# Block loads on GpSimd's DMA queue, an act's transposes inside the down product, and other paces for the side pieces

## The chip, the cores and the metric

One core of one Trainium2 chip runs the kernel. The metric is the device time of one execution in microseconds (us); the median of several runs counts. 0.2% of it is 3.9 us.

## The reference, cut to what matters

A transformer layer stack on 256 tokens of width 2048, in float32: a mixer (gated linear attention and dilated attention), a feed-forward part, a second mixer (retention and convolution), and a sliding-window attention. The change touches the feed-forward part alone:

```python
D_MODEL = 2048; SEQ = 256; FFN_HIDDEN = 5632
h = rms_norm(x, g2)
act = silu(h @ w_gate) * (h @ w_up)      # w_gate, w_up: 2048 x 5632
x = x + act @ w_down                     # w_down: 5632 x 2048
```

## The kernel before, in words

**Products.** A float32 product is made of three TensorE products: each operand is split into a high and a low half (`split`, L162 on ScalarE casts the high half `hi`, L163 on VectorE subtracts to get the low half `lo`), and `three` (L187 to L189) adds x_hi·w_hi, x_hi·w_lo and x_lo·w_hi into one PSUM bank. "A half" below is such a `lo` row on VectorE (DVE). Weights come from HBM in raw tiles of 128 x 2 x 512 (512 KB, five of them, `rows` at L126 issues them on SyncE's queue, SP); four `hi` and four `lo` tiles. `linear` makes an output block of 256 x 512: 8 steps for every 512 rows of the weight, each step one call of `three` for one of the two 128-row halves of the tokens, and after each step a call of `deal()`.

**The feed-forward part** goes over 11 column blocks of 512 (NB). `plain(j)` computes column block j by `linear` over w_gate and w_up: SiLU of the first product, then the product row L556 (twice, one for each 128 tokens) makes the act, and `act_done` transposes it (8 transposes, L545, into PSUM tiles `tr`) and splits it into the operand pair `mh`, `ml` of the down product. `seven(j)` computes another column block by a scheme of seven block products in place of eight; its work isn't called at once but put into a queue of side pieces, `side`, from which `deal()` takes one every `pace[0]` steps of the running `linear`: 12 `first` pieces (a raw load, split, products) and then 16 `rest` pieces. A `rest` piece subtracts one 128 x 2 x 512 block of weights from another in place (L668, on DVE), splits the result and multiplies. `ahead` loads these blocks into a ring of six tiles (two named b in the raw pool, two in the pool of the act pairs, u10 and u11), one to two pieces ahead: a block's load can be issued only when the last reader of the tile six blocks earlier, a half on DVE, is through. The result banks of `rest` are the PSUM tiles named `at` and one `acc`.

**The order.** There are five rounds: `seven(2w+1)` fills the queue, `plain(2w+2)` runs (64 steps), and `down` (64 steps) multiplies two acts by w_down in four column blocks (`x_add`, L254, adds them to x), the side pieces being dealt into all of it; `drain` runs what is left. One round is 128 steps. The tile framework's scheduler then sets the final order on each engine from the program's order and its dependences; the excerpts below are of that final order. In it, u10 and u11 are printed as `u_...` and the first four tiles of the ring as `b_...`, with a running number.

Of the kernel before, what the change touches and what calls it, by code (L numbers as in the profile page):

```python
# [18 lines left out]
P = 128  # L19
# [61 lines left out]
def model(ctx, tc, a, out):  # L81
    nc = tc.nc
# [14 lines left out]
    def nm(s):  # L97
        cnt[0] += 1
        return f"{s}{cnt[0]}"
# [4 lines left out]
    def unit(i, shape, dtype=F32):  # L104
        return wk.tile([P] + list(shape), dtype, tag=f"u{i}", name=nm(f"u{i}_"))
# [15 lines left out]
    def raw_tile():  # L121
        return raw_p.tile([P, 2, 512], F32, tag="raw", name=nm("raw"))

    def rows(dst, w, k, c0, n=512):

        nc.sync.dma_start(dst[:, :, :n], w[k * P:(k + 2) * P, c0:c0 + n].rearrange("(k p) f -> p k f", p=P))  # L126

    def fetch(w, kg, c0, n):

        raws = [raw_tile() for _ in range(2)]  # L130
        for i in range(2):
            rows(raws[i], w, 4 * kg + 2 * i, c0, n)
        return raws
# [26 lines left out]
    def split(hi, lo, src, scale=None):  # L160
        if scale is None:
            A.copy(hi, src)  # L162
            V.tensor_tensor(lo, src, hi.bitcast(F32), ALU.subtract)  # L163
        else:
            A.activation(hi, src, AF.Copy, scale=scale)
            V.scalar_tensor_tensor(lo, src, scale, hi.bitcast(F32), ALU.mult, ALU.subtract)

    def pair(pool, tag, **kw):
        return (pool.tile([P, 4, S], F32R, tag=tag + "h", name=nm(tag + "h"), **kw),
                pool.tile([P, 4, S], F32R, tag=tag + "l", name=nm(tag + "l"), **kw))  # L170
# [6 lines left out]
    pace = [1, 0]  # L177

    def deal():
        if side:  # L180
            pace[1] += 1
            if pace[1] >= pace[0]:
                pace[1] -= pace[0]
                side.popleft()()

    def three(o, xh, xl, hi, lo, start, stop):
        T.matmul(o, xh, hi, start=start, stop=False)  # L187
        T.matmul(o, xh, lo, start=False, stop=False)  # L188
        T.matmul(o, xl, hi, start=False, stop=stop)  # L189

    def linear(w, c0, n, groups, got=(), fine=False):
        accs = [ps_acc.tile([P, 512], F32, tag="acc", name=nm("acc")) for _ in range(2)]
        for gi, ((xh, xl), kg) in enumerate(groups):
            raws = got[gi] if gi < len(got) else fetch(w, kg, c0, n)
            for k in range(4):
                k2 = k % 2
                if k2 == 0:
                    raw = raws[k // 2]
                    hi = hl_p.tile([P, 2, 512], F32R, tag="hi", name=nm("hi"))
                    lo = hl_p.tile([P, 2, 512], F32R, tag="lo", name=nm("lo"))  # L200
                    if fine and gi == 0:
                        for j in range(2):
                            split(hi[:, j, :n], lo[:, j, :n], raw[:, j, :n])
                    else:
                        split(hi[:, :, :n], lo[:, :, :n], raw[:, :, :n])
                for t in range(2):
                    o = accs[t][:, :n]
                    st, en = gi == 0 and k == 0, gi == len(groups) - 1 and k == 3
                    sl = slice(t * P, (t + 1) * P)
                    three(o, xh[:, k, sl], xl[:, k, sl], hi[:, k2, :n], lo[:, k2, :n], st, en)  # L210
                    deal()
        return accs
# [35 lines left out]
    def full(st):  # L248
        return [(st["T"][b], b) for b in range(4)]

    def x_add(b, accs):
        for t in range(2):
            xs = x[:, t, b * 512:(b + 1) * 512]
            V.tensor_tensor(xs, xs, accs[t], ALU.add)  # L254
# [61 lines left out]
    for b in range(4):  # L316
        xh, xl = st["T"][b] = pair(xt_p, "x")
# [13 lines left out]
    got = first  # L331
    for c0, n in ((2688, 400), (2304, 384), (2048, 256)):
        accs = linear(w_in, c0, n, full(st), got, fine=n == 400)
        got = []
# [91 lines left out]
    for vb in range(2):  # L426
# [4 lines left out]
        for hh in range(2):  # L431
# [19 lines left out]
            for t in range(2):  # L451
                o = po[:, t * S:(t + 1) * S]
                T.matmul(o, aT[:, t], v[:, t, vs], start=True, stop=True)
                for c in range(2):
                    n = 2 * t + c
# [69 lines left out]
    w_gate, w_up, w_down = a["w_gate"][0], a["w_up"][0], a["w_down"][0]  # L525
# [3 lines left out]
    acts = {}  # L529
    nst = new_stream()  # L530

    def down(bs, last):
        for b in range(4):
            x_add(b, linear(w_down, b * 512, 512, [(acts[j], j) for j in bs]))
            if last:
                x_done(nst, b, NEV)

    def act_done(j, sg):
        ah, al = acts[j] = pair(mt_p, "m")
        for i in range(2):  # L540
            ps = ps_w.tile([P, 512], F32, tag="w", name=nm("tr"))
            for k in range(2):
                for t in range(2):
                    c = (2 * i + k) * P
                    T.transpose(ps[:, k * S + t * P:k * S + (t + 1) * P], sg[:, t, c:c + P], ident)  # L545
            split(ah[:, 2 * i:2 * i + 2].rearrange("p c s -> p (c s)"),
                  al[:, 2 * i:2 * i + 2].rearrange("p c s -> p (c s)"), ps)

    def plain(j):
        ag = linear(w_gate, j * 512, 512, full(st))  # L550
        sg = unit(4, [2, 512])
        for t in range(2):
            silu_gate(sg[:, t], ag[t], rh[:, t:t + 1])
        au = linear(w_up, j * 512, 512, full(st))
        for t in range(2):
            V.scalar_tensor_tensor(sg[:, t], au[t], r2h[:, t:t + 1], sg[:, t], ALU.mult, ALU.mult)  # L556
        act_done(j, sg)

# [66 lines left out]
    def seven(j):  # L627

        c0 = j * 512
        c = {}  # L630

        def first(kp, n):
            if kp == 0:
                c[n] = work_bank()
            raw = raw_tile()
            rows(raw, (w_gate, w_up, w_gate)[n], (0, 8, 8)[n] + 2 * kp, c0)
            times(c[n], ("A11", "S4", "A12")[n], parts(raw), kp)
            if n == 2:
                ahead(0, kp)
            if kp < 3:  # L640
                return
            if n < 2:
                c["p", n] = temp("Lx", 4)
                A.copy(c["p", n], c[n])
                return
            sg = c["sg"] = unit(5, [2, 512])
            c11 = temp("junk2", 3)
            V.tensor_tensor(c11, c["p", 0], c[2], ALU.add)
            silu_gate(sg[:, 0], c11, rh[:, 0:1])

        def ahead(kp, n):

            if kp > 3:
                return
            for i in ((0, 1), (), (2,), (3,))[n]:
                b = c["b", kp, i] = block_tile()
                rows(b, (w_up, w_gate, w_up, w_gate)[i], (0, 0, 8, 8)[i] + 2 * kp, c0)

        def rest(kp, n):
            ahead(kp + 1, n)  # L660
            if n == 0:
                if kp == 0:
                    pace[0] = 5.75
                    c["P"] = [work_bank() for _ in range(3)] + [ps_acc.tile([P, 512], F32, tag="acc", name=nm("acc"))]
            b12, b11, b22, b21 = [c["b", kp, i] for i in range(4)]
            dst, x0, x1, which = ((b11, b12, b11, "S1"), (b12, b22, b12, "S3"), (b22, b22, b11, "S2"),
                                  (b21, b22, b21, "A22"))[n]
            V.tensor_tensor(dst, x0, x1, ALU.subtract)  # L668
            times(c["P"][n], which, parts(dst), kp)
            if kp == 3 and n == 3:  # L670
                last()

        def last():
            b5, b7, b6, b4 = c["P"]
            p1, p3, sg = c["p", 0], c["p", 1], c["sg"]
            V.tensor_tensor(p1, p1, b6, ALU.add)
            c12, c21 = temp("junk2", 3), temp("junk2", 3)
            V.tensor_tensor(c12, p1, b5, ALU.add)
            V.tensor_tensor(p1, p1, b7, ALU.add)
            V.tensor_tensor(c21, p1, b4, ALU.subtract)  # L680
            V.tensor_tensor(p1, p1, b5, ALU.add)
            V.tensor_tensor(c12, c12, p3, ALU.add)
            silu_gate(sg[:, 1], c21, rh[:, 1:2])
            for t, cu in enumerate((c12, p1)):
                V.scalar_tensor_tensor(sg[:, t], cu, r2h[:, t:t + 1], sg[:, t], ALU.mult, ALU.mult)
            act_done(j, sg)


        pace[0] = 1.75
        side.extend([lambda kp=kp, n=n: first(kp, n) for kp in range(4) for n in range(2)])  # L690
        side.extend([lambda kp=kp: first(kp, 2) for kp in range(4)])
        side.extend([lambda kp=kp, n=n: rest(kp, n) for kp in range(4) for n in range(4)])

    def drain():
        while side:
            side.popleft()()
        pace[0] = 1

    plain(0)
    left_sums()  # L700
    for w in range(5):
        seven(2 * w + 1)
        plain(2 * w + 2)
        down([2 * w - 1, 2 * w + 2] if w else [0, 2], False)
        drain()
    down([9], True)
    st = nst
# [74 lines left out]
    for half in range(2):  # L782
# [15 lines left out]
        for c in range(4):  # L798
            i = 4 * half + c
# [202 lines left out]
    for g in range(4):  # L1002
# [4 lines left out]
        sg = unit((0, 4)[g % 2], [2, 512])  # L1007
# [53 lines left out]
```

## Time and profile before

| | |
|---|---|
| median of 3 runs | 1927.17 us (1927.04 to 1930.02) |
| the profiled execution | 1926.19 us, its span 1924.4 us |
| TensorE (PE) busy | 1906.0 us, 99% |
| VectorE (DVE) busy | 1276.6 us, 66% |
| ScalarE (ACT) busy | 968.9 us, 50% |
| GpSimd (POOL) busy | 201.1 us, 10% |
| bytes read from HBM | 384 MB, 201 GB/s over the span |

Times in the profile are counted from the start of the span. The feed-forward part lies between about 400 and 1105 us. A row of the timeline gives the start, the time, the engine, the line of the kernel, the operation with its output and inputs, and in brackets how long the engine stood idle before it and what ended the wait. The views used are the busy table, the busy time in a window, the lists of waits by engine, the timelines of single engines, the times from issue to landing of one tile's DMAs, and the list of DMA issues.

### The profile page before, as it was taken

Reading aid. Unit: us, or ns where it says so; the run is one execution under the profiler, and the core shown is the slowest. Engines: PE = TensorE matmul, PEld = TensorE weight load, DVE = VectorE, ACT = ScalarE, POOL = GpSimd, SP = SyncE. Lnnn points to the kernel's source line nnn. Section 1 sums busy time; section 2 is a strip of 40 time slices with the busy share of each in tenths; the row PEclk is TensorE's granted clock in tenths of the full one; section 3 lists DMA queues with packets and bytes.
Section 4 is the critical chain, followed back from the end, with each engine's and each line's share of the span. In section 5 each row is a group of like instructions: output and inputs, shape, how many; then the busy total and the mean of one; then the engine's idle time right before and its main releaser. Section 6 shows DMA issues by size and latency. Waiting matters only on the chain.

```text
span 1924.4 us, 23805 instructions
## 1 busy us (share of the span) xinstructions
PE 1906.0 (99%) x8808; PEld 1567.0 (81%) x8808; DVE 1276.6 (66%) x1486; ACT 968.9 (50%) x1313; POOL 201.1 (10%) x315
## 2 busy tenths in 40 slices
PE   8999999999999999999999999999999999999999
PEld 8877888888778888788787888888888888878787
DVE  6454555587787887787887875555555666677654
ACT  6544545465546546455455454444444354566542
POOL 1000222110000000000000110100000003754100
PEclk9999999999999999999999999999999999999999
DMA  8675665567768778677687656566666556544464
GB/s 306 198 209 152 186 175 165 166 207 249 247 223 276 233 227 272 221 259 240 229 268 238 191 165 192 159 196 169 191 188 191 191 179 188 170 132 132 146 202 134
DMA packets 202724, 387.72 MB, mean 201 GB/s; under 512 B 12312, under 2 KB 20528, under 8 KB 202480
## 3 DMA queue, kind: packets, MB, share of 16 engines
q1 hardware_dynamic: 201472, 382.12, 64.3%
q0 software_dynamic: 992, 4.03, 0.7%
q8 instruction: 69, 1.13, 0.2%
q14 instruction: 47, 0.39, 0.1%
q10 hardware_dynamic: 144, 0.05, 0.0%
HBM read 384.04 MB, written 3.68 MB: 201 GB/s over the span
## 4 chain that ended last, share of the span: by engine, by line
PE 89%; DMA 4%; DVE 4%; issue 1%; POOL 1%; ACT 0%; SPq 0%; DVEq 0%; ACTq 0%
PE acc L188 25%; PE acc L187 25%; PE acc L189 25%; PE at L188 2%; PE at L189 2%; PE at L187 2%; DVE lo L163 2%; DMA b<-in_w_up_dram 2%; DMA b<-in_w_gate_dram 1%; PE at L960 1%; DVE b L668 1%; DMA u<-in_w_up_dram 1%; PE tr L225 1%; PE tr L307 1%; DMA u<-in_w_gate_dram 0%
## 5 line engine op out<-in xcount | busy, mean ns | idle before, releaser
L163 DVE TENSOR_TENSOR lo<-raw,hi 128x1024 fp32r<-128x1024 f32 (+3 forms) x646 | 786.4, 1224 | 464.8 <-ACT hi L162 460.2
L162 ACT CAST hi<-raw 128x1024 fp32r<-128x1024 f32 (+3 forms) x646 | 669.4, 1040 | 664.8 <-PE acc L189 561.5
L188 PE MATMUL acc<-lo,xh 128*128 128x512 f32 (+3 forms) x1640 | 637.2, 389 | 0.4 <-DVE lo L163 0.4
L189 PE MATMUL acc<-hi,xl 128*128 128x512 f32 (+3 forms) x1640 | 636.2, 388 | 0.0
L187 PE MATMUL acc<-hi,xh 128*128 128x512 f32 (+3 forms) x1640 | 622.7, 390 | 5.7 <-ACT hi L162 5.7
L187 PEld LDWEIGHTS acc<-hi,xh 128*128 128x128 f32 x1640 | 308.2, 188 | 68.8 <-ACT hi L162 6.0
L188 PEld LDWEIGHTS acc<-lo,xh 128*128 128x128 f32 x1640 | 308.9, 188 | 64.1 <-issue 3.3
L189 PEld LDWEIGHTS acc<-hi,xl 128*128 128x128 f32 x1640 | 309.0, 188 | 59.5 <-issue 0.4
L188 PE MATMUL acc<-lo,mh 128*128 128x512 f32 x640 | 251.0, 392 | 0.0
L189 PE MATMUL acc<-hi,ml 128*128 128x512 f32 x640 | 249.0, 393 | 0.0
L187 PE MATMUL acc<-hi,mh 128*128 128x512 f32 x640 | 247.1, 393 | 1.0 <-ACT mh L162 1.0
L187 PEld LDWEIGHTS acc<-hi,mh 128*128 128x128 f32 x640 | 120.5, 188 | 27.1 <-DVE x L254 1.5
L188 PEld LDWEIGHTS acc<-lo,mh 128*128 128x128 f32 x640 | 120.3, 188 | 25.7 <-DVE lo L163 1.8
L189 PEld LDWEIGHTS acc<-hi,ml 128*128 128x128 f32 x640 | 119.8, 188 | 24.4
L162 ACT CAST hi<-b 128x1024 fp32r<-128x1024 f32 x54 | 56.9, 1054 | 74.5 <-PE acc L189 47.3
L163 DVE TENSOR_TENSOR lo<-b,hi 128x1024 fp32r<-128x1024 f32 x54 | 65.9, 1221 | 4.8 <-ACT hi L162 3.9
L668 DVE TENSOR_TENSOR b<-b,b 128x1024 f32<-128x1024 f32 x41 | 50.1, 1222 | 28.3 <-DMA b<-in_w_gate_dram 13.5
L720 POOL DMA_DIRECT2D u<-in_c_even_dram x1 | 0.6, 633 | 651.9 <-PE at L189 651.9
L254 DVE TENSOR_TENSOR x<-x,acc 128x512 f32<-128x512 f32 x88 | 57.7, 681 | 9.9 <-PE acc L189 9.8
L188 PE MATMUL at<-lo,u 128*128 128x512 f32 x160 | 63.5, 397 | 0.4 <-DVE lo L163 0.3
L189 PE MATMUL at<-hi,u 128*128 128x512 f32 x160 | 62.4, 390 | 0.0
L187 PE MATMUL at<-hi,u 128*128 128x512 f32 x160 | 62.4, 390 | 0.0
(253 smaller groups left out, 1567.1 us busy)
## 6 DMA issues: line engine op xcount, KB each, us to landing
raw<-in_ev_w_in_dram SPq DMA_DIRECT2D x128, 512.0 KB, 3.9
raw<-in_w_gate_dram SPq DMA_DIRECT2D x88, 512.0 KB, 4.5
raw<-in_w_down_dram SPq DMA_DIRECT2D x88, 512.0 KB, 5.1
raw<-in_w_in_dram SPq DMA_DIRECT2D x80, 512.0 KB, 3.8
raw<-in_od_w_in_dram SPq DMA_DIRECT2D x72, 512.0 KB, 3.7
raw<-in_w_up_dram SPq DMA_DIRECT2D x68, 512.0 KB, 4.7
raw<-in_w_out_dram SPq DMA_DIRECT2D x32, 512.0 KB, 3.6
raw<-in_ev_w_out_dram SPq DMA_DIRECT2D x32, 512.0 KB, 3.7
```

What stands on the lines that cost most here:

```text
L162: A.copy(hi, src)
L163: V.tensor_tensor(lo, src, hi.bitcast(F32), ALU.subtract)
L187: T.matmul(o, xh, hi, start=start, stop=False)
L188: T.matmul(o, xh, lo, start=False, stop=False)
L189: T.matmul(o, xl, hi, start=False, stop=stop)
L225: T.transpose(ps[:, k * S + t * P:k * S + (t + 1) * P], x[:, t, c:c + P], ident)
L254: V.tensor_tensor(xs, xs, accs[t], ALU.add)
L307: T.transpose(ps[:, k * S + t * P:k * S + (t + 1) * P], src(t)[:, c:c + P], ident)
L668: V.tensor_tensor(dst, x0, x1, ALU.subtract)
L720: nc.gpsimd.dma_start(ce, a["c_even"][:, :512])
L960: T.matmul(pv[e * 64:(e + 1) * 64, :S], vo[:, k, g * 64:(g + 1) * 64], PT[:, :, e], start=k == 0, stop=k == t)
```

## The change

`rows` takes the queue as an argument, and `ahead` issues its blocks on GpSimd's queue, in the program's order. `plain` no longer transposes its act: it returns a function, which `down` calls (as `mid`) in its first column block before the second group of eight steps. `down` reads `acts[j]` when it comes to the group. The paces become 2.5 steps for the `first` pieces and 5.1 for the `rest` pieces (1.75 and 5.75 before). The rows L556, L545, L668 and L254 of before are L559, L548, L672 and L257 in the changed kernel.

```diff
@@ -121,9 +121,9 @@
     def raw_tile():
         return raw_p.tile([P, 2, 512], F32, tag="raw", name=nm("raw"))
 
-    def rows(dst, w, k, c0, n=512):
-
-        nc.sync.dma_start(dst[:, :, :n], w[k * P:(k + 2) * P, c0:c0 + n].rearrange("(k p) f -> p k f", p=P))
+    def rows(dst, w, k, c0, n=512, queue=nc.sync):
+
+        return queue.dma_start(dst[:, :, :n], w[k * P:(k + 2) * P, c0:c0 + n].rearrange("(k p) f -> p k f", p=P))
 
     def fetch(w, kg, c0, n):
 
@@ -188,9 +188,12 @@
         T.matmul(o, xh, lo, start=False, stop=False)
         T.matmul(o, xl, hi, start=False, stop=stop)
 
-    def linear(w, c0, n, groups, got=(), fine=False):
+    def linear(w, c0, n, groups, got=(), fine=False, mid=None):
         accs = [ps_acc.tile([P, 512], F32, tag="acc", name=nm("acc")) for _ in range(2)]
-        for gi, ((xh, xl), kg) in enumerate(groups):
+        for gi, (pr, kg) in enumerate(groups):
+            if gi == 1 and mid is not None:
+                mid()
+            xh, xl = pr() if callable(pr) else pr
             raws = got[gi] if gi < len(got) else fetch(w, kg, c0, n)
             for k in range(4):
                 k2 = k % 2
@@ -529,9 +532,9 @@
     acts = {}
     nst = new_stream()
 
-    def down(bs, last):
+    def down(bs, last, mid=None):
         for b in range(4):
-            x_add(b, linear(w_down, b * 512, 512, [(acts[j], j) for j in bs]))
+            x_add(b, linear(w_down, b * 512, 512, [(lambda j=j: acts[j], j) for j in bs], mid=mid if b == 0 else None))
             if last:
                 x_done(nst, b, NEV)
 
@@ -554,7 +557,7 @@
         au = linear(w_up, j * 512, 512, full(st))
         for t in range(2):
             V.scalar_tensor_tensor(sg[:, t], au[t], r2h[:, t:t + 1], sg[:, t], ALU.mult, ALU.mult)
-        act_done(j, sg)
+        return lambda: act_done(j, sg)
 
 
 
@@ -654,13 +657,14 @@
                 return
             for i in ((0, 1), (), (2,), (3,))[n]:
                 b = c["b", kp, i] = block_tile()
-                rows(b, (w_up, w_gate, w_up, w_gate)[i], (0, 0, 8, 8)[i] + 2 * kp, c0)
+                tc.keep_in_program_order(rows(b, (w_up, w_gate, w_up, w_gate)[i], (0, 0, 8, 8)[i] + 2 * kp, c0,
+                                              queue=nc.gpsimd))
 
         def rest(kp, n):
             ahead(kp + 1, n)
             if n == 0:
                 if kp == 0:
-                    pace[0] = 5.75
+                    pace[0] = 5.1
                     c["P"] = [work_bank() for _ in range(3)] + [ps_acc.tile([P, 512], F32, tag="acc", name=nm("acc"))]
             b12, b11, b22, b21 = [c["b", kp, i] for i in range(4)]
             dst, x0, x1, which = ((b11, b12, b11, "S1"), (b12, b22, b12, "S3"), (b22, b22, b11, "S2"),
@@ -686,7 +690,7 @@
             act_done(j, sg)
 
 
-        pace[0] = 1.75
+        pace[0] = 2.5
         side.extend([lambda kp=kp, n=n: first(kp, n) for kp in range(4) for n in range(2)])
         side.extend([lambda kp=kp: first(kp, 2) for kp in range(4)])
         side.extend([lambda kp=kp, n=n: rest(kp, n) for kp in range(4) for n in range(4)])
@@ -696,12 +700,12 @@
             side.popleft()()
         pace[0] = 1
 
-    plain(0)
+    plain(0)()
     left_sums()
     for w in range(5):
         seven(2 * w + 1)
-        plain(2 * w + 2)
-        down([2 * w - 1, 2 * w + 2] if w else [0, 2], False)
+        mid = plain(2 * w + 2)
+        down([2 * w - 1, 2 * w + 2] if w else [0, 2], False, mid)
         drain()
     down([9], True)
     st = nst
```

**Place 1, DVE in the first round, around the product row.** In the kernel before (the `lo` rows are halves of blocks, b_ and u_, and of raw tiles):

```order
L668 TENSOR_TENSOR u_890_4346<-u_885_4314,u_890_4346 128x1024
L163 TENSOR_TENSOR lo_4334<-raw_4301,hi_4333 128x1024
L163 TENSOR_TENSOR lo_4350<-b_4189,hi_4349 128x1024
L163 TENSOR_TENSOR lo_4387<-raw_4382,hi_4386 128x1024
L163 TENSOR_TENSOR lo_4403<-raw_4383,hi_4402 128x1024
L668 TENSOR_TENSOR b_4411<-b_4409,b_4411 128x1024
L556 SCALAR_TENSOR_TENSOR u_848_4133<-acc_4138,r2h_3443,u_848_4133 128x512
L556 SCALAR_TENSOR_TENSOR u_848_4133<-acc_4139,r2h_3443,u_848_4133 128x512
L163 TENSOR_TENSOR lo_4415<-b_4234,hi_4414 128x1024
```

and in the changed kernel:

```order
L672 TENSOR_TENSOR u_887_4336<-u_887_4336,b_4267 128x1024
L163 TENSOR_TENSOR lo_4358<-raw_4353,hi_4357 128x1024
L672 TENSOR_TENSOR u_898_4380<-u_887_4336,u_898_4380 128x1024
L163 TENSOR_TENSOR lo_4374<-raw_4354,hi_4373 128x1024
L559 SCALAR_TENSOR_TENSOR u_838_4103<-acc_4108,r2h_3443,u_838_4103 128x512
L559 SCALAR_TENSOR_TENSOR u_838_4103<-acc_4109,r2h_3443,u_838_4103 128x512
L163 TENSOR_TENSOR lo_4384<-b_4225,hi_4383 128x1024
L163 TENSOR_TENSOR lo_4423<-raw_4418,hi_4422 128x1024
L163 TENSOR_TENSOR lo_4438<-b_4267,hi_4437 128x1024
L163 TENSOR_TENSOR lo_4454<-raw_4419,hi_4453 128x1024
L672 TENSOR_TENSOR b_4434<-b_4432,b_4434 128x1024
L163 TENSOR_TENSOR ml_4403<-tr_4404,mh_4402 128x512
```

Before, the two product rows (L556) stood behind the subtraction of b_4411; now they (L559) stand ahead of the subtraction of b_4434, and behind this one stands the half of the transposed act (ml_4403).

**Place 2, TensorE (PE) in the same stretch, around the act's transposes.** Before (acc_4380 and acc_4381 are the down product's banks, at_4068 one of the `rest` products):

```order
L187 MATMUL acc_4380<-hi_4402,mh_3745 128x512
L188 MATMUL acc_4380<-lo_4403,mh_3745 128x512
L189 MATMUL acc_4380<-hi_4402,ml_3746 128x512
L187 MATMUL at_4068<-hi_4414,u_763_3789 128x512
L545 MATMUL tr_4366<-cm,u_848_4133 128x128
L187 MATMUL acc_4381<-hi_4386,mh_3745 128x512
```

and in the changed kernel (acc_4352 is a bank of the down product, acc_4128 of the `rest` products):

```order
L187 MATMUL acc_4352<-hi_4373,mh_3745 128x512
L188 MATMUL acc_4352<-lo_4374,mh_3745 128x512
L189 MATMUL acc_4352<-hi_4373,ml_3746 128x512
L548 MATMUL tr_4404<-cm,u_838_4103 128x128 x4
L188 MATMUL acc_4128<-lo_4384,xh_3310 128x512
L189 MATMUL acc_4128<-hi_4383,xl_3311 128x512
L187 MATMUL acc_4128<-hi_4383,xh_3310 128x512
```

The first transpose stood 13 matmuls behind the first matmul of the down product; it now stands 25 matmuls behind it, with 31 matmuls between it and the last of the up product (18 before).

**Place 3, the queues that issue the block loads, first round.** SP before:

```order
L126 DMA u_885_4314<-in_w_up_dram 128x2x512
L126 DMA raw_4433<-in_w_down_dram 128x2x512
L126 DMA raw_4434<-in_w_down_dram 128x2x512
L126 DMA b_4409<-in_w_up_dram 128x2x512
L126 DMA raw_4484<-in_w_down_dram 128x2x512
L126 DMA b_4411<-in_w_gate_dram 128x2x512
L126 DMA raw_4485<-in_w_down_dram 128x2x512
```

and GpSimd (POOL) in the changed kernel:

```order
L126 DMA u_887_4336<-in_w_up_dram 128x2x512
L126 DMA u_898_4380<-in_w_gate_dram 128x2x512
L126 DMA b_4432<-in_w_up_dram 128x2x512
L126 DMA b_4434<-in_w_gate_dram 128x2x512
L126 DMA b_4504<-in_w_up_dram 128x2x512
L126 DMA b_4544<-in_w_gate_dram 128x2x512
```

The blocks stood among the raw loads on SP; now they follow one another on GpSimd's queue, and SP issues raw loads alone.

## Rows read from the trace of the kernel before

**Rows 1.** The page: span, busy time of each engine, TensorE's granted clock in 40 slices.

```profile
span 1924.4 us, 23805 instructions
...
PE 1906.0 (99%) x8808; PEld 1567.0 (81%) x8808; DVE 1276.6 (66%) x1486; ACT 968.9 (50%) x1313; POOL 201.1 (10%) x315
...
PEclk9999999999999999999999999999999999999999
```

**Rows 2.** Windows: the feed-forward part, busy time (instructions) by engine, clock, DMA share, GB/s.

```profile
400.00:1110.00 710.00, 703.27 (x3127) 575.29 (x3126) 571.70 (x568) 374.00 (x391) 14.39 (x24) 1.00 0.74 238
```

**Rows 3.** Waits of PE, 400 to 1100 us: total us, times, longest us.

```profile
PE tr L545 <- DVE u L556: 5.3, 4, 1.9
PE at L188 <- DVE lo L163: 0.3, 1, 0.3
```

**Rows 4.** Timeline of DVE, 505 to 580 us: start, us, row, idle before it.

```profile
515.94 1.23 DVE L668 TENSOR_TENSOR b<-u,b 128x1024 f32<-128x1024 f32 x1 [3.12 <-DMA u<-in_w_up_dram]
...
518.35 1.22 DVE L163 TENSOR_TENSOR lo<-b,hi 128x1024 fp32r<-128x1024 f32 x1
...
521.75 1.22 DVE L163 TENSOR_TENSOR lo<-b,hi 128x1024 fp32r<-128x1024 f32 x1
...
528.53 1.23 DVE L668 TENSOR_TENSOR b<-b,b 128x1024 f32<-128x1024 f32 x1 [3.29 <-DMA b<-in_w_gate_dram]
...
539.97 1.23 DVE L668 TENSOR_TENSOR b<-b,b 128x1024 f32<-128x1024 f32 x1 [2.33 <-DMA b<-in_w_up_dram]
541.12 1.22 DVE L163 TENSOR_TENSOR lo<-u,hi 128x1024 fp32r<-128x1024 f32 x1
...
568.24 1.22 DVE L163 TENSOR_TENSOR lo<-raw,hi 128x1024 fp32r<-128x1024 f32 x1
...
577.64 1.22 DVE L163 TENSOR_TENSOR lo<-raw,hi 128x1024 fp32r<-128x1024 f32 x1
```

**Rows 5.** Timeline of PE, places between 520 and 580 us.

```profile
520.50 0.39 PE L188 MATMUL at<-lo,u 128*128 128x512 f32 x1
...
524.29 0.39 PE L188 MATMUL acc<-lo,xh 128*128 128x512 f32 x1
...
542.39 0.50 PE L188 MATMUL at<-lo,u 128*128 128x512 f32 x1 [0.29 <-DVE lo L163]
...
569.51 0.50 PE L188 MATMUL acc<-lo,mh 128*128 128x512 f32 x1
...
578.99 0.42 PE L188 MATMUL acc<-lo,mh 128*128 128x512 f32 x1
```

**Rows 6.** Waits of SP's queue, 400 to 1100 us.

```profile
SPq L126 <- DVE lo L163: 549.6, 311, 6.9
```

**Rows 7.** Timeline of SP's queue, 505 to 525 us.

```profile
508.96 0.37 SPq L126 DMA_DIRECT2D raw<-in_w_down_dram  x1
510.09 0.37 SPq L126 DMA_DIRECT2D u<-in_w_up_dram  x1
...
523.00 0.37 SPq L126 DMA_DIRECT2D b<-in_w_gate_dram  x1
```

**Rows 8.** Timeline of all engines, 160 to 163 us: DVE and GpSimd.

```profile
161.23 0.88 DVE L281 SCALAR_TENSOR_TENSOR og<-at,fq,u 128x256 f32<-128x256 f32 x2 [2.44 <-ACT u L430]
...
162.41 0.87 POOL L466 DMA_DIRECT2D u<-skew  x1 [1.21 <-DVE og L281]
```

**Rows 9.** Tile u, 161 to 167 us: its DMA (GpSimd's load of the skewed tile).

```profile
DMA to landing us min/median/max: 4.2/4.2/4.2
```

**Rows 10.** Tile raw, 155 to 159 us: its DMAs (SP).

```profile
DMA to landing us min/median/max: 3.6/3.7/3.8
```

**Rows 11.** DMA issues, whole span: tile, queue, count, KB each, median us to landing.

```profile
raw<-in_w_in_dram SPq DMA_DIRECT2D x80, 512.0 KB, 3.8
...
b<-in_w_up_dram SPq DMA_DIRECT2D x27, 512.0 KB, 4.9
...
u<-skew POOLq DMA_DIRECT2D x2, 512.0 KB, 4.8
```

## The prediction, made before the changed kernel was run

> **What bounds the kernel now.** I began with the busy table and the clock line: TensorE is busy for 1906.0 of 1924.4 us and its granted clock reads 9 (90% or more of 2.4 GHz) in all 40 slices [rows 1]. So time can be won only where TensorE idles, and lost wherever something new makes it idle. The change touches the feed-forward part alone, so next comes the window over it: 703.27 us busy out of 710 [rows 2]. The idle there, 6.7 us, is the ceiling of any gain. The list of TensorE's waits says what it is made of: 5.3 us in four waits of a transpose for the product it transposes, and one wait of 0.3 us for a low half [rows 3]. 0.2% of this kernel is 3.9 us, about what a measurement of it can tell from no change; a gain can hardly be seen unless it takes nearly all of that.
>
> A busy TensorE with few waits need not have much margin, so I read the timelines next. DVE is not full, but it halts at the in-place subtractions, for blocks still landing: 3.12 us at 515.94, 3.29 us at 528.53 [rows 4]. What stands behind such a subtraction in DVE's order is late too. TensorE's rows show how late: the low half ending at 542.34 (541.12 + 1.22) is used at 542.39, that ending at 569.46 at 569.51, that ending at 578.86 at 578.99 [rows 4, 5]. Each stands right behind a block's subtraction, and the margins are 0.05, 0.05 and 0.13 us. After the subtraction at 515.94 it is 0.93 us: a half ending at 519.57, used at 520.50. **The block's path (buffer free, issue, landing, subtraction, low half) already ends within a tenth of a microsecond of TensorE's need at three places a round.**
>
> **The queue.** SP waits 549.6 us in total for low halves to free buffers [rows 6]; such waiting cost nothing unless a block stood behind it. It did not: the half at 521.75 ends at 522.97, and SP issues the block that takes its buffer at 523.00, 0.03 us later [rows 4, 7]. The Trainium skill (DMA: Bandwidth & Descriptors, "Issuing engines are not separate DMA queues") says that issuing from several engines saves only the time of issuing; by it at most those 0.03 us are to be had, and the trace agrees as far as it goes.
>
> What GpSimd's queue costs: the only 512 KB loads of that queue beside ordinary work are the two of the skewed tile. DVE's pair ends at 162.11 and GpSimd's DMA row starts at 162.41 [rows 8]: 0.30 us, 0.27 more than SP. That load landed in 4.2 us [rows 9]; SP's loads just before it in 3.6 to 3.8 [rows 10]. The two skew loads show 4.8, SP's loads of that stage 3.8 [rows 11]. So a block comes later by 0.27 + 0.4 = 0.67 us at the near end and 0.27 + 1.0 = 1.27 at the far end. There is a lower end: a block now stands on SP's queue behind whatever raw load went before it (508.96, then the block at 510.09) [rows 7], and blocks land in 4.9 us where undisturbed loads take 3.8 [rows 11]; a queue of its own could win those 1.1 us, which makes it 0.67 − 1.1 = −0.4. I take **0.7**: the engines that move the bytes are the same, and a raw load already under way still holds them.
>
> The Trainium skill has a fit for loads by this queue (same page, "Anatomy of one DMA — SWDGE (gpsimd) path": 2.0 us plus the bytes at 436 GB/s). An estimate by it is 3.2 us for 512 KB, less than SP's 3.8; with it the sum below would come to about 1925 (a block 0.33 us earlier, as in rival 2 below). The row has 4.2, so the measurement decides.
>
> **The transposes.** Before, the product of the plain act (L556) stood behind the subtraction of b_4411, which waited 3.29 us [rows 4]; that made the transposes late. In the new order the two products stand ahead of the next waiting subtraction (b_4434), and 31 matmuls lie between the last of the up product and the first transpose. At 703.27 / 3127 = 0.225 us each [rows 2] that is 7.0 us, and two products take 1.4. The four waits go: **−5.3 us**. What is late next is the half that the transposes themselves make: ml_4403 stands behind b_4434's subtraction, and TensorE needs it some 19 matmuls (4.3 us) after its first use of the half (lo_4384) that frees b_4434's buffer.
>
> **The terms, per round** (each is positive only if the margin is used up; 0.7 us is the later block):
> - A, subtraction of b_4265 with u_887 (before: b_4232 with u_885, at 515.94). Between the freeing half's first use and the next need lie 25 matmuls where 32 lay, 1.6 us less. 0.93 − 1.6 − 0.7 = −1.37. But that load was slow: 510.09 to 515.94 is 5.85 us, and blocks land in 4.9 by the median [rows 11], so I give 0.86 back: 0.5 us lost.
> - B, subtraction of b_4434. From the end of the freeing half: 0.03 + 0.7 + 4.9 + 0.1 (landing to start), one subtraction 1.14 and the transposes' half 0.69, together 7.56 us. Against it stand 4.3 us of matmuls and the lead that DVE had when the freeing half ended. Soon after a late subtraction that lead is small: the half that ended at 522.97, three DVE rows behind the one at 518.35, was used at 524.29 [rows 5], 1.3 us later. With 1.3: 1.96 us lost.
> - C, the next subtraction of the ring (before at 539.97, ahead of 541.12) [rows 4]: margin 0.05, cover 1 matmul less: 0.87 lost; half given back for the slower load of that round: 0.6.
> - D, the one before 554: cover grows by five matmuls (1.1 us). Nothing.
> - E, ahead of 569.51: same cover, margin 0.05: 0.65. F, ahead of 578.99: margin 0.13: 0.57. These two belong to blocks of the next round, so they come four times.
>
> Sum: 5 × (0.5 + 1.96 + 0.6) + 4 × (0.65 + 0.57) = 15.3 + 4.9 = 20.2 us, less 5.3: **+14.9 us**.
>
> Costed at nothing: the pieces' pace (12 × 2.5 + 16 × 5.1 = 111.6 steps where there were 113; DVE has 138 us of room in the 710) [rows 2]. Raw loads without blocks on SP: they hardly held TensorE up. Blocks on GpSimd keep their program order, so one that used to overtake (u_890 ahead of u_885) is issued up to 0.9 us behind it; its subtraction is the third behind the late one, 3.5 us on. GpSimd's statistics now stand ahead of the first block, about 420 us; the four to six blocks there come in a burst, and DVE may wait 3 to 4 us once, against a lead of as much: nothing, at most 2 us.
>
> The profiled execution took 1926.2 us against a median of 1927.2, within the spread. **1926.2 + 14.9 = 1941.1.**
>
> **Rivals.**
> 1. *The block comes earlier on a queue of its own* (−0.4). A, C, E and F vanish; B is 7.56 − 1.1 − 4.3 = 2.16 us against DVE's lead. From a lead of 2.16 on nothing is lost and the gain stands: 1920.9, at best 1919.5 (all 6.7 us idle gone). For it: 4.9 against 3.8. Against it: SP issues further raw loads one or two microseconds behind a block (523.00 is followed by two, as the order shows), which queued behind it before and will now share the engines with it. Chance 0.20.
> 2. *The parts cancel.* With a lead of 1.3 and a block later by 0, B costs 1.26 × 5 = 6.3 and nothing else does: 1927.2. At 0.2 later the losses are 8.7: 1929.6; at −0.4 they are 4.3: 1925.2. Chance 0.19.
> 3. *The block loses its place ahead of the later raw loads.* By the same rows the traffic costs a load up to 1.1 us; half of it on top of the far end makes 1.27 + 0.5. Each microsecond costs 5 × 3 + 4 × 2 = 23 us, so 1.07 more than my 0.7 gives 1941 + 25 = 1966; 1.27 alone gives 1954. The Trainium skill (same page, "SWDGE vs HWDGE vs iDMA") has each DMA engine take turns between the two kinds of queue, which is how this would come about; no row of before shows two such loads side by side. Chance 0.14.
> 4. *The transposes still wait:* the product could stand behind another late subtraction, u_898 two rows ahead. Its block is issued right behind u_887's and has 3.5 us more to land, so I count this in the others' width.
>
> **How the numbers follow.** My case, 1931 to 1954 by a block 0.27 to 1.27 later: 0.47. With rival 3 slower has 0.61; same (rival 2) 0.19; faster (rival 1) 0.20. The range from 1920 to 1957 takes in the bounds and most of rivals 1 and 2; above it lies a part of rival 3, below it the last microsecond.
>
> **What would show it.** Right: no wait of a transpose for the product; GpSimd's DMA rows start 0.3 us behind the freeing half; blocks land in over 5 us; TensorE's waits for low halves (acc, at and tr products) grow from 0.3 to about 20 us, the largest single kind behind b_4434's subtraction. Wrong: blocks that land in under 4.5 us, or TensorE's idle in the feed-forward part still near 7 us or below it.

## The result and the profile after

The changed kernel takes 1937.5 us (median of 4 runs, 1934.7 to 1938.5); the kernel before, beside it, 1927.1 us. The ratio is 1.0052, with an interval of 1.0040 to 1.0064: slower by 10.4 us. The profiled execution took 1937.5 us with a span of 1935.7 us, 11.3 us more than the span before.

The page's first lines and the window over the feed-forward part, which is about 10 us longer now, so that it ends at 1120:

```profile
span 1935.7 us, 23806 instructions
...
PE 1908.9 (99%) x8808; PEld 1566.6 (81%) x8808; DVE 1276.9 (66%) x1486; ACT 971.0 (50%) x1313; POOL 261.7 (14%) x395
```

```profile
400.00:1120.00 720.00, 705.56 (x3120) 574.81 (x3119) 573.14 (x568) 375.47 (x391) 76.25 (x104) 1.00 0.73 236
```

TensorE does the same work (8808 matmuls), and its idle time in this part goes from 6.7 us [rows 2] to 14.4 us. GpSimd's 60.6 us more are nearly all the issues of the 80 blocks (0.72 us each). TensorE's waits in 400 to 1110 us (total, times, longest) show what became of the 5.3 us [rows 3]:

```profile
PE acc L188 <- DVE lo L163: 7.9, 9, 1.9
PE acc L189 <- DVE xl L166: 3.0, 1, 3.0
PE tr L548 <- DVE ml L163: 1.6, 3, 0.7
```

No transpose waits for its product any more. In its place TensorE waits for low halves, 9.5 us together, and once for 3.0 us on a low part (`xl`) of the normalized x. That one wait belongs to the first blocks. On DVE, PE and GpSimd:

```profile
428.48 1.23 DVE L672 TENSOR_TENSOR b<-b,b 128x1024 f32<-128x1024 f32 x1 [7.68 <-DMA b<-in_w_gate_dram]
...
430.76 0.87 DVE L166 SCALAR_TENSOR_TENSOR xl<-tr,gc,xh 128x256 fp32r<-128x256 f32 x2
```

```profile
431.30 1.00 PE L189 MATMUL acc<-hi,xl 128*128 128x512 f32 x2 [3.03 <-DVE xl L166]
```

```profile
421.13 0.22 POOL L530 TENSOR_SCALAR r2h<-st_r 128x2 f32<-128x2 f32 x1
421.34 0.80 POOL L126 DMA_DIRECT2D b<-in_w_up_dram  x1
422.14 0.73 POOL L126 DMA_DIRECT2D b<-in_w_gate_dram  x1
```

The first blocks are issued behind GpSimd's statistics, four in a row (SP had issued the last of them at 409.30 before), and DVE halts 7.68 us for the second of them with work for TensorE queued behind. The windows before and behind the stall show a second cost:

```profile
428.20:431.30 3.10, 0.07 (x2) 0.01 (x1) 2.82 (x4) 0.00 (x0) 0.00 (x0) 1.00 0.38 149
431.30:435.30 4.00, 4.00 (x11) 3.17 (x12) 4.00 (x5) 1.05 (x1) 0.00 (x0) 0.57 0.55 143
435.30:440.00 4.70, 4.70 (x22) 3.88 (x21) 4.70 (x5) 3.31 (x4) 0.00 (x0) 1.00 0.63 187
```

After the idle 3.1 us TensorE ran at a granted clock of 0.57 for 4.0 us, most of it at its 1.2 GHz level: 11 matmuls where 4.0 us at 0.225 us each hold 18. That is another 1.6 us, an estimate.

The largest of the other waits comes at one place, four times in all (for the first blocks of the second to fifth round): 1.86, 1.24, 1.32 and 1.04 us (5.5 us). Its first instance, on GpSimd's queue, SP's queue, the tile (landing), DVE and PE:

```profile
552.78 0.72 POOL L126 DMA_DIRECT2D u<-in_w_gate_dram  x1 [8.49 <-DVE lo L163]
```

```profile
551.38 0.37 SPq L126 DMA_DIRECT2D raw<-in_w_down_dram  x1
```

```profile
553.64 0.37 SPq L126 DMA_DIRECT2D raw<-in_w_down_dram  x1
```

```profile
DMA to landing us min/median/max: 6.5/6.5/6.5
```

```profile
559.43 1.23 DVE L672 TENSOR_TENSOR u<-u,u 128x1024 f32<-128x1024 f32 x1 [4.68 <-DMA u<-in_w_gate_dram]
```

```profile
561.85 0.50 PE L188 MATMUL acc<-lo,mh 128*128 128x512 f32 x1 [1.86 <-DVE lo L163]
```

The block has raw loads of SP close ahead and close behind (551.38, 553.64) and takes 6.5 us to land. In the list of DMA issues the blocks' medians are:

```profile
b<-in_w_up_dram POOLq DMA_DIRECT2D x27, 512.0 KB, 5.4
b<-in_w_gate_dram POOLq DMA_DIRECT2D x27, 512.0 KB, 5.6
```

against 4.9 for the first before [rows 11]. From the end of the freeing half to GpSimd's row it was 0.30 us wherever GpSimd was free, as at the skewed tile [rows 8].

### The profile page after: what moved, and what is told of

The parts are those of the page before. It is cut to its first block, busy times and chain, and to the rows that moved or that the text cites. A ratio compares the mean times of both kernels' runs of the same rounds, so it can differ in the third digit from the quotient of the medians.

```text
span 1935.7 us, 23806 instructions
## 1 busy us (share of the span) xinstructions
PE 1908.9 (99%) x8808; PEld 1566.6 (81%) x8808; DVE 1276.9 (66%) x1486; ACT 971.0 (50%) x1313; POOL 261.7 (14%) x395
## 4 chain that ended last, share of the span: by engine, by line
PE 76%; issue 10%; DMA 5%; DVE 5%; POOL 3%; ACT 1%; SPq 0%; DVEq 0%; POOLq 0%; ACTq 0%
PE acc L189 22%; PE acc L188 22%; PE acc L187 22%; DVE lo L163 3%; DMA b<-in_w_gate_dram 3%; PE at L188 1%; PE at L189 1%; PE at L187 1%; DMA u<-in_w_gate_dram 1%; POOL b L126 1%; PE at L964 1%; PE tr L310 1%; PE tr L228 0%; POOL u L126 0%; DMA b<-in_w_up_dram 0%
## 5 line engine op out<-in xcount | busy, mean ns | idle before, releaser
L672 DVE TENSOR_TENSOR b<-b,b 128x1024 f32<-128x1024 f32 x41 | 50.1, 1222 | 31.7 <-DMA b<-in_w_gate_dram 23.1
L257 DVE TENSOR_TENSOR x<-x,acc 128x512 f32<-128x512 f32 x88 | 56.9, 681 | 9.9 <-PE acc L189 9.8
L126 POOL DMA_DIRECT2D b<-in_w_up_dram x27 | 19.6, 725 | 265.1 <-DVE lo L163 265.1
```

What stands on the lines that cost most here:

```text
L126: return queue.dma_start(dst[:, :, :n], w[k * P:(k + 2) * P, c0:c0 + n].rearrange("(k p) f -> p k f", p=P))
```

## The experiments

The theory after this reading: the order of the changed kernel gains the 5.3 us, and GpSimd's queue costs more than that. The rival (P): the new paces, and the order that follows from them, cost the time. A change to the source is not a change of one thing here, since the scheduler makes a new final order from it; so the first four runs change one part of the source each, and the later ones hold the order.

**One part at a time.** Blocks back on SP (e1):

```diff
-                tc.keep_in_program_order(rows(b, ..., c0, queue=nc.gpsimd))
+                rows(b, (w_up, w_gate, w_up, w_gate)[i], (0, 0, 8, 8)[i] + 2 * kp, c0)
```

> The changed kernel with the block loads back on SP's queue (unpinned, as before); transposes and paces as changed. Theory (GpSimd's queue is what costs, the moved transposes gain): the feed-forward part idles about 1 us, near 1921.5 us, a ratio to the kernel before of 0.996 to 0.998. Rival P (the new paces and the order that follows from them cost the time): stays slower than before, 1930 us or more.

Measured: 1943.9 us, ratio 1.0089 (1.0075 to 1.0102). The theory's number is missed by 22 us, and the kernel is slower than with the blocks on GpSimd. PE's waits over the feed-forward part (20.4 us with one of 1.0 us for `mh`):

```profile
PE acc L188 <- DVE lo L163: 10.5, 8, 1.9
PE tr L548 <- DVE ml L163: 4.7, 5, 1.4
PE at L188 <- DVE lo L163: 4.2, 4, 1.4
```

The queue alone, on the kernel before (e2), with the edit of `rows` and `ahead` from the change and nothing else:

> The kernel before with only the block loads moved to GpSimd's queue, pinned. Theory: all of the queue's cost and none of the gain, with the products still behind a subtraction that waits longer: 1940 us or more (1938 to 1950), transposes' wait for the product above 8 us. Rival P: no more than 1932.

Measured: 1953.4 us, ratio 1.0130 (1.0111 to 1.0149). The time is 3 us above the range expected; the transposes' wait is 6.7 us, less than expected.

The transposes alone (e3: the changed kernel with the blocks on SP and the paces 1.75 and 5.75):

> The kernel before with only the plain act's transposes moved into the down product. Theory: the four waits of 5.3 us go, 1921 to 1923 us. Rival G (the gain is given back by the half of the transposed act, late behind the subtraction): 1926 to 1928.

Measured: 1927.7 us, ratio 1.0001 (0.9992 to 1.0010): rival G's number, but not by its mechanism. PE's list has

```profile
PE acc L187 <- DVE u L559: 7.1, 5, 1.8
```

The product rows still stand behind the waiting subtraction. They also free the PSUM banks that the down product writes next, so its first matmul waits for them instead of the transposes. Moving the transposes gave nothing here, where the product stayed late.

The paces alone (e4: 2.5 and 5.1 in the kernel before):

> The kernel before with only the paces 2.5 and 5.1. Theory: within 2 us of before, 1925 to 1929. Rival P: 1932 or more.

Measured: 1944.2 us, ratio 1.0088 (1.0075 to 1.0102): rival P's number. PE waits for low halves in two lines, and in one window of the first round, behind two waits of 0.71 and 1.88 us, the clock is again low:

```profile
PE acc L188 <- DVE lo L163: 9.6, 6, 1.9
PE at L188 <- DVE lo L163: 3.4, 4, 1.2
```

```profile
528.40:532.00 3.60, 3.60 (x11) 2.72 (x10) 3.24 (x4) 0.00 (x0) 0.00 (x0) 0.56 0.95 280
```

The clock falls so in each of the five rounds of e4 (0.54 to 0.59 in the 3.6 us from 528.40, 661.40, 793.80, 926.90 and 1060.00) and five times in e2, for one:

```profile
642.00:646.00 4.00, 4.00 (x12) 3.14 (x12) 3.25 (x3) 1.05 (x1) 0.72 (x1) 0.59 0.79 237
```

At the 1.6 us above for each, an estimate, that is some 8 us of e4's 17 and of e2's 26. In e1's rounds, where nearly the same waits stand, it stays at 1.00: e1 idles 20.4 us, e4 14.0, and they take the same time.

So the paces cost 17 us by themselves and the queue 26 us, but together with the transposes only 10: the parts don't add. In e1 one subtraction stands a half earlier in DVE's order than in the changed kernel (b_4265 ahead of lo_4340, not behind it), and the next two follow without a half of a raw tile between:

```
L671 TENSOR_TENSOR b_4265<-u_887_4336,b_4265 128x1024
L163 TENSOR_TENSOR lo_4340<-b_4193,hi_4339 128x1024
L671 TENSOR_TENSOR u_887_4336<-u_887_4336,b_4267 128x1024
L671 TENSOR_TENSOR u_898_4380<-u_887_4336,u_898_4380 128x1024
L163 TENSOR_TENSOR lo_4358<-raw_4353,hi_4357 128x1024
```

The first of them waits for its block, and both halves are late behind them (PE waits 1.07 us for lo_4340, 1.87 for lo_4358):

```profile
521.28 1.23 DVE L671 TENSOR_TENSOR b<-u,b 128x1024 f32<-128x1024 f32 x1 [4.46 <-DMA u<-in_w_up_dram]
```

```profile
527.23 0.51 PE L188 MATMUL acc<-lo,mh 128*128 128x512 f32 x1 [1.87 <-DVE lo L163]
```

**The order held.** The next kernels add, at the end of the trace, an edge from each instruction to the next on PE, DVE and ACT, from a table that holds another kernel's final order:

```diff
     with tile.TileContext(nc, schedule_with_timeline_sim=True) as tc:
         model(tc, aps, out)
+        hold(tc)      # for x, y in zip(names, names[1:]): tc.add_manual_dep(ins[y], x, NoSync)
```

Blocks on SP in the changed kernel's order (f1):

> The changed kernel with the block loads on SP's queue, and PE, DVE and ACT held to the changed kernel's own final order, so that the queue alone differs. Theory Q (in this order the queue costs about 5 us at the first blocks and 6 us where a raw load shares the engines, and gains about 1 us a round where a block no longer stands behind raw loads): 1930 to 1934 us. Rival O (the queue gains, and the slower run with blocks on SP owed nothing to its other order): 1940 us or more.

Measured: 1920.7 us, ratio 0.9962 (0.9950 to 0.9975), faster than both kernels and than either expectation. The code is that of e1, and the final order alone is worth 23.2 us between the two. PE's whole list of waits in 400 to 1100 us, and the blocks' landing:

```profile
PE acc L187 <- ACT mh L162: 1.0, 1, 1.0
```

```profile
b<-in_w_up_dram SPq DMA_DIRECT2D x27, 512.0 KB, 4.8
b<-in_w_gate_dram SPq DMA_DIRECT2D x27, 512.0 KB, 4.5
```

With PE, DVE and ACT in one and the same order, the queue costs 1935.7 − 1918.9 = 16.8 us by the spans, and the order gains 1924.4 − 1918.9 = 5.5 us. The 16.8 us hold what pinning costs, too: on SP the blocks aren't pinned, and some overtake (in the first round SP issues a w_gate block at 511.49, ahead of the w_up block at 513.76 that stands before it in the program). That share was not measured. Rival P falls as the cause of the changed kernel's loss: its paces and its order gain. It holds for e1 and e4, where the scheduler made other orders.

The queue in the order of the kernel before (f2, blocks not pinned):

> The kernel before with the block loads on GpSimd's queue, not pinned, and PE, DVE and ACT held to the order of the kernel before. Theory: margins of 0.05 to 0.13 us are used up in every round and the products stay behind the late subtraction: 1938 to 1948 us. Rival: the 26 us of the queue alone came from the order that the scheduler made of it, and here it is within 5 us of before.

Measured: 1966.0 us, ratio 1.0202 (1.0181 to 1.0223), 18 us above the range expected. PE's first line of waits, and the landing of the block whose subtraction stands ahead of the product (issued at 530.04; before, 5.4 us at 523.00):

```profile
PE tr L545 <- DVE u L556: 19.8, 5, 4.3
```

```profile
DMA to landing us min/median/max: 6.9/6.9/6.9
```

Over the five rounds this block took 7.4 us on average (6.87 to 7.58) where it took 5.3 before. SP issues one raw load 1.4 us ahead of it (528.63) and two right behind it (at 530.90 and 532.03); before, one stood ahead of it and two behind it in the same line. Two other things are in the time. The clock is low in and behind the transposes' wait in all five rounds, in the third:

```profile
810.90:818.30 7.40, 5.33 (x14) 4.19 (x15) 5.99 (x6) 1.04 (x1) 0.72 (x1) 0.54 0.27 72
```

And, not pinned, the first two blocks are issued at 3.31 and 4.08 us, among the kernel's first loads (on SP at 10.60 and 11.57 before): in the first 400 us TensorE does 1860 matmuls where it did 1877, some 4 us by an estimate at 0.225 us each.

The first four blocks on SP, the rest on GpSimd, in the changed kernel's order (f3):

```diff
-                                              queue=nc.gpsimd))
+                first = j == 1 and kp == 0
 ...
+                         queue=nc.sync if first else nc.gpsimd)
```

> The changed kernel in its own order, the first four blocks of the first round on SP (issued early there), all others on GpSimd. Theory: the one stall of 3.0 us at 431 us and the 4 us at half clock behind it go: 4.8 us less than the changed kernel, about 1932.7 us. Rival: the stall comes later instead, no less than 1936 us.

Measured: 1934.3 us, ratio 1.0031 (1.0020 to 1.0043). Its span and the changed kernel's differ by 3.2 us, between the two expectations. The 3.0 us wait is gone from the list, but the others grew by 1.6 us together:

```profile
PE acc L188 <- DVE lo L163: 8.7, 11, 2.1
PE tr L548 <- DVE ml L163: 2.4, 4, 1.4
```

The order of before with only the two product rows moved ahead of the one waiting subtraction in each round (g1):

```diff
 (DVE's order, five places)
-L668 b_4411 / L556 / L556
+L556 / L556 / L668 b_4411
```

> The kernel before in its own order, but in each of the five rounds the two product rows of the plain act moved ahead of the one waiting subtraction in DVE's order; queue, transposes and paces as before. Theory: the product fits into the 3.3 us in which DVE waits for the block, the transposes' waits of 5.3 us go and nothing takes their place: 1920 to 1922.5 us. Rival G (given back, as with the transposes moved alone): 1926 us or more.

Measured: 1922.1 us, ratio 0.9967 (0.9954 to 0.9979). The number is the theory's, though a little comes back at the half behind that subtraction:

```profile
PE at L188 <- DVE lo L163: 2.3, 4, 1.2
```

**Whose queue?** Two kernels in the order of before ask whether a block is late because GpSimd issues it, or because it shares the DMA engines with loads of another queue. Raw loads of the down product on GpSimd (but for the last call of `down`), blocks on SP (f4), and both on GpSimd (f5); the line of f4:

```diff
-            x_add(b, linear(w_down, ..., [(acts[j], j) for j in bs]))
+            x_add(b, linear(w_down, ..., [(acts[j], j) for j in bs], queue=nc.sync if last else nc.gpsimd))
```

> The kernel before with PE, DVE and ACT held to its own order, blocks on SP as before, but the raw loads of the down product on GpSimd's queue. Theory S (what costs a block most is sharing the engines with raw loads issued behind it on another queue, whichever queue is whose): the block of the subtraction ahead of the product (slot 13 of 16) lands in 5.5 us or more although it is on SP, against 5.3 before where it stood behind one raw load and ahead of two, and the transposes' wait for the product stays at 5 us or more. Rival D (it is GpSimd's own writing of descriptors): that block lands in 4.6 us or less, and the transposes' wait goes below 3 us.

Measured: 1935.5 us, ratio 1.0045 (1.0030 to 1.0060). The block named (slot 13) landed in 5.0 us on average and the transposes waited 3.1 us, both between the two expectations, so it decides nothing; it no longer had a raw load ahead of it in its own line. But the block after it, on SP too, with a raw load of GpSimd issued 0.9 us ahead (532.10) and another behind, took this long from its issue at 533.03:

```profile
DMA to landing us min/median/max: 6.9/6.9/6.9
```

against 5.4 us at 534.58 before, where it stood behind one raw load of its own queue. Over the rounds it is 6.2 against 4.9, and PE's waits moved there:

```profile
PE at L188 <- DVE lo L163: 6.4, 4, 1.9
PE tr L545 <- DVE u L556: 3.1, 5, 1.1
```

So a block that SP issues can be delayed by the other queue as well. In four rounds a raw load of GpSimd was issued 0.9 us ahead of this block and one 1.6 to 1.7 us behind it, and it took 6.3 to 7.0 us; in the other round none stood ahead, two 0.5 and 1.6 us behind, and it took 4.1.

> The same held order, with the blocks and the raw loads of the down product both on GpSimd's queue, so that they stand in one line again. Theory S: the block of slot 13 lands in 4.5 to 5.8 us where it took 7.4 with the blocks alone on GpSimd, the transposes wait 6 to 12 us in all instead of 19.8, the time is 1932 to 1945 us instead of 1966. Rival D: that block still lands in 6.5 us or more and the time stays above 1955 us.

Measured: 1959.2 us, ratio 1.0160 (1.0143 to 1.0177). The landing is as theory S says, 5.6 us on average for slot 13 where it was 7.4, and the transposes wait 11.6 us where it was 19.8:

```profile
PE tr L545 <- DVE u L556: 11.6, 5, 2.5
PE acc L188 <- DVE lo L163: 9.4, 13, 2.3
PE at L188 <- DVE lo L163: 4.8, 6, 1.9
```

The time is not: the expectation was 1932 to 1945 us, and rival D's above 1955. Low halves cost 14.2 us elsewhere in this kernel (9.0 in f2), and the first 400 us, again with two blocks among the first loads, some 5 us (1855 matmuls for 1877). With raw loads and blocks both later, other subtractions come late; which share of that is the raw loads' was not measured.

## Why the prediction was right, and where its steps were not

**The outcome.** Forecast: 1941.1 us, slower by 14.9; measured: 1937.5, slower by 10.4. Of the two halves, the gain of 5.3 us is 5.5 us by f1, and the loss of 20.2 us is 16.8 us. Of its signs, the waits for the product went, GpSimd's rows started 0.3 us behind the freeing half, and blocks landed in over 5 us; the waits for low halves grew to 9.5 us and not to about 20, and the largest are not behind b_4434's subtraction.

**The gain** came as the step said: the products stand ahead of the waiting subtraction, and the four waits are gone. g1 shows that this alone does it, and e3 that the moved transposes do not.

**The later block** was put at 0.7 us. The first part (0.27 us to the issue) was right: 0.30 against 0.03 us. The landing grew by 0.5 us in the median of w_up's blocks (5.4 against 4.9), so the sum is 0.8. As an average it hides a spread from 4.1 to 7.5 us: in the same order (f1) the block of A lands later on SP, behind a raw load (5.5 us against 4.9), and that of D earlier (5.0 against 6.1). That is rival 1 and rival 3 at once, and the terms went wrong by it (idle times of PE in the timeline of after, over all rounds, and 1.6 us for the clock at the first blocks):

| term | forecast | measured |
|---|---|---|
| A | 2.5 | 1.1 |
| B | 9.8 | 1.9 |
| C | 3.0 | 0 |
| D | 0 | 5.5 |
| E | 2.6 | 1.4 |
| F | 2.3 | 0.5 |
| first blocks | 0, at most 2 | 4.6 |

They make 15.0 us; f1 idles 0.8 us in the same stretch (both without 1.0 us for `mh`), so they explain some 14 of the 16.8 us. A wait also costs more than its idle time: rows of 0.39 us start 0.225 us apart where nothing waits, and the idle time is counted from the end of the row before. At up to 0.17 us for each of the dozen waits that f1 does not have, an estimate, that is 2 us more.

**The step that failed** is D: "cover grows by five matmuls (1.1 us). Nothing." It took the landing from the old order, where this block landed in 3.6 to 3.8 us, and priced the queue by the same 0.7 us as for all others. In the new order a raw load is issued 1.1 us ahead of it, and even on SP (f1) it lands in 5.0 us on average. That uses up the cover: the half behind its subtraction is ready 0.06 to 0.25 us before TensorE needs it, in the first of the four cases at 555.62 for 555.74:

```profile
554.40 1.22 DVE L163 TENSOR_TENSOR lo<-raw,hi 128x1024 fp32r<-128x1024 f32 x1
```

```profile
555.74 0.43 PE L188 MATMUL acc<-lo,mh 128*128 128x512 f32 x1
```

On GpSimd the block takes 6.1 us, 1.1 more, and 0.27 more to the issue, and nearly all of that is lost, 1.4 us each time. (A raw load of SP behind it did not delay a block by itself: with one 0.9 us behind and none closer than 2.5 us ahead, blocks of the changed kernel landed in 4.2 to 4.7 us, B's among them; D's have one 1.4 us ahead as well.)

A, B and C went the other way. A's block landed in 4.9 us on average where its round before had 5.8. B's and C's landed in 4.5 and 4.4 us where the sum had 4.9 and some of the 0.7; that was the new order and not the queue, since on SP in the same order they took 4.3 and 4.5. B's lead was 1.9 to 2.1 us in place of 1.3 as well, since the transposes stand ahead of the first use of the freeing half (it ends at 531.73):

```profile
530.52 1.21 DVE L163 TENSOR_TENSOR lo<-b,hi 128x1024 fp32r<-128x1024 f32 x1
```

```profile
533.84 0.47 PE L188 MATMUL acc<-lo,xh 128*128 128x512 f32 x1
```

That the total came out near is luck: these errors have opposite signs.

**The first blocks** were seen (DVE may wait 3 to 4 us) but set against a lead that was not there: DVE waited 7.68 us, for the second of four loads in a row, which took 6.2 us to land, and TensorE stood 3.0 us. The half clock behind it was not in the sum at all. Putting these blocks back on SP (f3) gave 3.2 us of the 4.6 back.

**Not seen at all:** that the parts of the change interact through the scheduler. The prediction read the final order of the changed kernel and so needed no rule for it, but a reader who costs the paces alone, or the queue alone, from the diff would have been far off (17 and 26 us).

**On sharing.** f2 against f5 differ in whether the down product's raw loads stand in the blocks' line or in another: 7.4 against 5.6 us for the same block. The Trainium skill (DMA: Bandwidth & Descriptors, "SWDGE vs HWDGE vs iDMA") says that the engines take turns between the two kinds of queue; that fits these landings and the 6.2 us of the later block in f4, though no run here shows the turns themselves. The Trainium skill's sentence that issuing from several engines saves only the issuing time (same page, "Issuing engines are not separate DMA queues"), on which the prediction drew, does not hold here: in one held order the second queue cost 16.8 us. What decides how late a block lands is not settled: with a load of the other queue close ahead and one close behind it took 5.9 to 7.6 us at three places (D's block, f2's, and f4's later one in four rounds), but slot 13 of f4, with loads 0.9 us ahead and 1.4 us behind, took 5.0.

## What to carry to other kernels

A single queue is also an order: an urgent load that moves to a queue of its own leaves the loads ahead of it, and loses its place ahead of those behind it, so look for each urgent load which loads are issued close to it on either side. Where a scheduler sets the final order, compare sources only with the order held, or a change of one number is a change of everything: the same code took 1943.9 and 1920.7 us here. And where TensorE waits, look for what stands in front of its producer: moving two rows ahead of one waiting subtraction gave 6 us by the medians, and the final order of the changed kernel with the blocks left on SP gave 7.5.

## What the hardware showed that was not expected

A granted clock of 0.54 to 0.60 appeared in windows of 3.6 to 7.4 us behind TensorE's idle times, and not always. In the changed kernel it came once, behind 3.03 us of idle; in e4 in every round, in the first behind waits of 0.71 and 1.88 us; in e2 behind waits of 1.98 and 2.61 us (0.59 and 0.60). In e1 waits of 1.07 and 1.87 us at the same place were followed by a clock of 1.00, and in e2 one of 3.16 us as well:

```profile
528.40:532.00 3.60, 3.60 (x18) 2.98 (x17) 3.50 (x4) 0.36 (x1) 0.00 (x0) 1.00 0.87 270
```

```profile
431.50:435.50 4.00, 3.92 (x17) 3.27 (x18) 4.00 (x6) 2.08 (x3) 0.00 (x0) 1.00 0.56 141
```

The first row is e1's window, with 18 matmuls where e4 has 11. What decides between them stays open; no run here was made for it.
